# Twenty output stores of a hybrid attention layer issued by GpSimd instead of the sync engine

## The chip, the cores and the metric

The kernel runs on one core of a Trainium2 chip. A core has five engines that run side by side, each with its own instruction queue that is worked off in order: TensorE (PE, matrix products and transpositions), VectorE (DVE), ScalarE (ACT), GpSimd (POOL), and SyncE (SP), which here does nothing but issue DMA transfers. ACT and POOL can issue DMA transfers too; these stand in the same queue as their arithmetic. Engines wait for each other and for the landing of a transfer through semaphores. The metric is the time of the device for one execution in microseconds (us).

## What is computed

One layer of a diffusion backbone, in float32: 1024 latent tokens with 256 context tokens ahead of them, model width 1024. The normalised and modulated tokens are projected once; four heads run a gated delta rule in both directions, four heads a retention in both directions. Both outputs are normalised and gated, joined, projected by `w_out` and added to x; then follows a SwiGLU feed-forward part (FFN). Cut to what matters here:

```python
o_gdn = rms_norm(o_f + o_b, gdn_norm_g) * jax.nn.silu(z...)
o_ret = head_group_norm(r_f + r_b, ret_norm_g) * jax.nn.silu(rg...)
y = jnp.concatenate([o_gdn.reshape(b, tl, W_GDN), o_ret.reshape(b, tl, W_RET)], axis=-1)
...
x = x + g1 * (y[:, CTX_LEN:] @ w_out[layer])
x = x + g2 * swiglu(modulate(rms_norm(x, norm_ffn_g[layer]), sh2, sc2), w_ffn_in[layer], w_ffn_out[layer])
return rms_norm(x, final_g)
```

## The kernel before

Tokens are held in blocks of 128 (one token per partition): blocks t = 0, 1 are the context, t = 2 to 9 the latent tokens, also called l = t − 2 = 0 to 7. A float32 product is made of three products of rounded parts (`hi*hi`, `lo*hi`, `hi*lo`).

The stages that the change touches run between about 630 and 850 us:

- **The delta-rule scan.** Ten steps, in each a forward block and a backward block (`steps`, `step`). When the second direction reaches a latent block, `gate(l)` squares the sum O on ACT into the tile `yo` (L959), makes the norm's factor, multiplies with the factor and the gate `zg` on DVE back into `yo` (L964), and stores `yo` into the first half of the row block `dy[l]` in HBM (L966): eight stores of 256 KB. `yo` has two buffers, so ACT's squares of a block wait until the store of two blocks before has landed. The loads of `zg` (L664, two buffers) wait for the multiply that reads the old one.
- **The retention.** `rstate` makes the state of a block (`kz` on POOL, L1021; `ru` on PE; `Rf` on DVE, L1031), `turn` the transposed queries and keys `qk` (ACT, L1060 and L1061; POOL, L1065 and L1066), `scores` the masked products `pm`, and `output(t)` the output: PE `ro` (L1081 to L1083), ACT copies it into `oc` (L1085), DVE takes the head statistics (`bst`), ACT normalises (L1096, one operation for each head), POOL multiplies with the gate (L1099), and the result is stored into the second half of `dy[t - 2]` (L1100). The blocks t = 2 to 5 run between the scan's steps and are stored from POOL; t = 6 to 9 run after it (`forward_tail`, here called the tail) and are stored from SP. In the rows below these four are oc_8171, oc_8252, oc_8333 and oc_8383.
- **The output projection.** `op_y(l)` loads both halves of `dy[l]` into `yt` (L664, two buffers), transposes them on PE (`yT`, L1187) and splits them into `yhi` (ACT) and `ylo` (DVE). `op_mm` multiplies with the parts of `w_out` (`wohi`, `wolo` and, for the second half of the columns, the tiles b11, t1 and so on; L1201 to L1203) and puts `x1` = x + g1·(y w_out) together on DVE (L1204, L1205). `op_norm(l)` stores `x1` into `dx1[l]` (L1211, 512 KB, read again at the very end of the kernel), takes its squares, and scales `x1` in place: the first half on DVE (L1215), the second on ACT (L1216). Both wait until the store has landed. PE then transposes `x1` (`x1T`, L1223), and its parts are combined on POOL for the FFN (L1237 and L1240, a burst of nine products for a block of the second half).
- **The FFN** begins with `ws` on POOL (L1315) and the split of the weights on ACT and DVE (`whi` L344, `wlo` L345).

The order of the instructions on each engine isn't written in the code: the framework's scheduler works it out with a timeline of its own before the kernel is built. Within an engine's queue the order is then fixed. An instruction that goes to another engine therefore also changes the order of its neighbours, on all engines.

Of the kernel before, what the change touches and what calls it, by code (L numbers as in the profile page):

```python
# [38 lines left out]
def build(nc, tc, ap, dbg=None, stop=None, marks=None):  # L39
    root = ExitStack()  # L40
    V, S, G, T, SY = nc.vector, nc.scalar, nc.gpsimd, nc.tensor, nc.sync
# [45 lines left out]
    def bank(tag, name):  # L87
        return PS["pool"].tile([P, 512], F32, tag=tag, name=name, bufs=PS["tags"][tag])

    def bank_a(name):  # L90
        return bank("pa", name)
# [99 lines left out]
    try:  # L191
# [698 lines left out]
        dy = dr.tile([LT, P, D], F32, tag="dy", name="dy")  # L890
# [62 lines left out]
        def gate(l):  # L953
            zg = zgs.pop(l)
            ssq = SC.tile([P, H], F32, tag="ssq", name="ssq")
            nqe = SC.tile([P, H], F32, tag="nqe", name="nqe")
            yo = SC.tile([P, H, P], F32, tag="yo", name="yo", bufs=2)
            for h in range(H):
                S.activation(yo[:, h, :], O[:, l, h, :], AF.Square, accum_out=ssq[:, h:h + 1])  # L959
            V.tensor_scalar(nqe, nq[:, l, :], P * EPS, P * EPS * EPS, ALU.mult, ALU.add)  # L960
            V.scalar_tensor_tensor(ssq, ssq, 1.0 / P, nqe, ALU.mult, ALU.add)
            rr = rsqrt_mean(SC, None, H, "rg", 0, ssq)
            for h in range(H):
                V.scalar_tensor_tensor(yo[:, h, :], O[:, l, h, :], rr[:, h:h + 1], zg[:, h * P:(h + 1) * P],  # L964
                                       ALU.mult, ALU.mult)
            SY.dma_start(dy[l, :, 0:512], yo.rearrange("p h v -> p (h v)"))  # L966

        zgs = {}

# [107 lines left out]
        def output(t, vv, gt, qk, pm, cur, tail):  # L1077
            po = bank_a("ro")
            for h in range(H):
                hs = slice(h * P, (h + 1) * P)  # L1080
                T.matmul(po[:, hs], qk[:, 2, h, :], cur[:, h, :], start=True, stop=False)  # L1081
                T.matmul(po[:, hs], qk[:, 3, h, :], rb[t][:, h, :], start=False, stop=False)
                T.matmul(po[:, hs], pm[:, h, :], vv[:, hs], start=False, stop=True)  # L1083
            oc = RT.tile([P, H, P], F32, tag="oc", name="oc", bufs=5)
            S.activation(oc.rearrange("p h v -> p (h v)"), po, AF.Copy)  # L1085
            bst = RT.tile([P, H, 6], F32, tag="bst", name="bst", bufs=2)
            mv = RT.tile([P, H, 2], F32, tag="mv", name="mv", bufs=2)
            for h in range(H):
                V.bn_stats(bst[:, h, :], oc[:, h, :])
            for h in range(H):  # L1090
                V.bn_aggr(mv[:, h, :], bst[:, h, :])
            rs = rsqrt_mean(RT, mv[:, :, 1], H, "rr", 1.0)
            nm_ = RT.tile([P, H], F32, tag="nm", name="nm", bufs=2)
            V.scalar_tensor_tensor(nm_, mv[:, :, 0], -1.0, rs, ALU.mult, ALU.mult)
            for h in range(H):
                S.activation(oc[:, h, :], oc[:, h, :], AF.Identity,  # L1096
                             bias=nm_[:, h:h + 1], scale=rs[:, h:h + 1])
            yf = oc.rearrange("p h v -> p (h v)")
            G.tensor_tensor(yf, yf, gt, ALU.mult)  # L1099
            (SY if tail else G).dma_start(dy[t - 2, :, 512:1024], yf)  # L1100

        def forward(t, cur):
            kk, vv, gt, qk = turn(t, False)
# [41 lines left out]
        def xhi(n, q, k=slice(0, 4)):  # L1145
            return X[n][:, 0, q, k, :]

        def xlo(n, q, k=slice(0, 4)):
            return X[n][:, 1, q, k, :]
# [25 lines left out]
        dx1 = dr.tile([LT, P, D], F32, tag="dx1", name="dx1")  # L1175
# [32 lines left out]

        def op_norm(l, y, tr=("pc", "pc")):
            _, _, xl, x1 = y  # L1210
            SY.dma_start(dx1[l], x1)  # L1211
            ssx = OP.tile([P, 1], F32, tag="ssx", name="ssx")
            S.activation(xl, x1, AF.Square, accum_out=ssx)
            rs = rsqrt_mean(OP, ssx, 1, "r1", D)
            V.tensor_scalar(x1[:, 0:512], x1[:, 0:512], rs, None, ALU.mult)  # L1215
            S.activation(x1[:, 512:1024], x1[:, 512:1024], AF.Copy, scale=rs)  # L1216
            sl = slice((l % 4) * P, (l % 4 + 1) * P)
            for half in range(2):
                pt = bank(tr[half], "x1T")
                hf = OP.tile([P, 4, P], F32, tag="hf", name="hf", bufs=4)  # L1220
                for i in range(4):
                    k = half * 4 + i
                    T.transpose(pt[:, i * P:(i + 1) * P], x1[:, k * P:(k + 1) * P], ident)  # L1223
                for i in range(4):
                    k = half * 4 + i
                    if l % 4 == 3 and i % 2:
                        S.activation(hf[:, i, :], pt[:, i * P:(i + 1) * P], AF.Identity,
                                     bias=ada2[:, 0, k:k + 1], scale=ada2[:, 1, k:k + 1])
                    else:
                        V.tensor_scalar(hf[:, i, :], pt[:, i * P:(i + 1) * P], ada2[:, 1, k:k + 1], ada2[:, 0, k:k + 1],  # L1230
                                        ALU.mult, ALU.add)
                held[l // 4, half] = hf
                e = V if l % 4 == 3 else G

                def part(n, src):
                    S.activation(xhi(n, l % 4), src, AF.Copy)
                    e.tensor_tensor(xlo(n, l % 4), src, xhi(n, l % 4).bitcast(F32), ALU.subtract)  # L1237

                def diff(n, r, p, q, op=ALU.subtract):
                    e.tensor_tensor(r, p, q, op)  # L1240
                    part(n, r)

                if l < 4:
                    part("b11" if half == 0 else "b21", hf)
                elif half == 0:
                    held["t1"] = OP.tile([P, 4, P], F32, tag="hs", name="hs", bufs=1)
                    diff("t1", held["t1"], hf, held[0, 0])
                else:
                    t1, b21, b12 = held["t1"], held[0, 1], held[1, 0]
                    diff("t2", t1, hf, t1)  # L1250
                    diff("t3", b12, hf, b12)
                    diff("t4", b21, b21, t1)
                    part("b22", hf)
# [4 lines left out]
        for i, l in enumerate(pairs):  # L1258
            y = nxt
            if l != 7:  # L1260
                nxt = op_y(pairs[i + 1])
            op_mm(y, int(l == 7))
            if before:
                op_norm(*before)
            op_mm(y, int(l != 7))
            before = l, y
# [281 lines left out]
        for m in (1, 6, 2, 7, 5, 4, 3):  # L1548
            gs = [list(range(j, min(j + 2, FH))) for j in range(4 if m == 1 else 0, FH, 2)]
            tail = 9 if m == 3 else 3  # L1550
# [104 lines left out]
```

## Time and profile before

| | us |
|---|---|
| runs shown | 1476.58, 1484.42, 1475.48 |
| their median | 1476.58 |
| the profiled execution, its own time | 1477.96 |
| its span in the trace | 1476.2 |

The profile is one execution, recorded on the chip. Busy times of the engines are sums over the span; a window gives the same for a stretch of it. A row of a group names the line of the kernel, the engine, the operation, what it writes and reads, how often it runs, and its durations. A row of the waits names who waited for whom, with the total in us, how often, and the longest. The chain of waits follows the last instruction back, at each step to what released it; its rows are start, duration and what ran. `SPq` and `POOLq` are the queues of these engines when they issue a transfer. DMA rows give the KB of one transfer and the median time from issue to landing. The names drop buffer numbers and trailing digits: `dx` is `dx1`, `x` can be `x1`.

### The profile page before, as it was taken

The page shows a single profiled execution, that of the slowest core. Times are in us where ns is not written, and L with a number is a line of the kernel's source. Part 1 is how long each engine was busy: PE and PEld are TensorE (multiplying, and loading weights), DVE is VectorE, ACT ScalarE, POOL GpSimd, SP SyncE. Part 2 cuts the span into 40 slices and gives each one's busy share as a digit, 9 for nine tenths or more (in the row PEclk, how much of TensorE's full clock was granted, in tenths as well). Part 3 has the DMA queues.
Part 4 walks back from the last instruction along what each step waited for, and adds up shares of the span by engine and source line. Part 5 has one row for each costly group of instructions (what it writes and reads, how often), then busy time and mean ns, then how long its engine had stood idle before and what let it go on. Part 6 is the DMA issues. An engine that isn't in the chain of part 4 may idle for free.

```text
span 1476.2 us, 24111 instructions
## 1 busy us (share of the span) xinstructions
PE 1397.2 (95%) x8919; PEld 1199.2 (81%) x8919; DVE 964.6 (65%) x1856; ACT 614.0 (42%) x1326; POOL 590.3 (40%) x501
## 2 busy tenths in 40 slices
PE   7999999986789999899799899999999999999997
PEld 2898888975689999898688688877888888788885
DVE  6566789289792435689676877556555564657477
ACT  5643564587333111245443623233333332444445
POOL 0120010243202344234144688898555552335321
PEclk9999999998899999999899999999999999999999
DMA  9536686688888625996532265674222242776863
GB/s 337 197 105 205 189 249 200 219 264 277 282 216 277 238 76 178 416 341 209 184 125 104 97 238 210 242 264 162 105 97 105 107 151 79 260 260 194 288 216 114
DMA packets 170421, 298.14 MB, mean 202 GB/s; under 512 B 43496, under 2 KB 93880, under 8 KB 165952
## 3 DMA queue, kind: packets, MB, share of 16 engines
q1 hardware_dynamic: 118752, 253.17, 50.2%
q10 hardware_dynamic: 49072, 35.83, 7.8%
q0 software_dynamic: 2480, 7.60, 1.4%
q8 instruction: 70, 1.15, 0.3%
q14 instruction: 47, 0.39, 0.1%
HBM read 206.60 MB, written 89.96 MB: 201 GB/s over the span
## 4 chain that ended last, share of the span: by engine, by line
PE 55%; POOL 6%; DMA 5%; DVE 4%; issue 2%; ACT 2%; SPq 1%; ACTq 0%; POOLq 0%; DVEq 0%
PE ffn L1344 7%; PE ffn L1342 6%; PE ffn L1343 6%; PE fo L1470 4%; PE fo L1469 4%; PE fo L1468 4%; PE tm L371 3%; PE tm L373 3%; PE tm L372 3%; PE op L1203 2%; PE op L1201 2%; PE op L1202 2%; DMA wd<-tw 2%; POOL ws L1315 1%; DMA pk<-sd 1%
## 5 line engine op out<-in xcount | busy, mean ns | idle before, releaser
L371 PE MATMUL tm<-whi,hhi 128*128 128x256 f32 (+1 forms) x704 | 199.5, 287 | 7.7 <-ACT vt L859 3.4
L372 PE MATMUL tm<-wlo,hhi 128*128 128x256 f32 (+1 forms) x704 | 199.3, 285 | 2.4 <-issue 2.0
L373 PE MATMUL tm<-whi,hlo 128*128 128x256 f32 (+1 forms) x704 | 197.7, 285 | 0.0
L371 PEld LDWEIGHTS tm<-whi,hhi 128*128 128x128 f32 x704 | 132.8, 190 | 11.8 <-ACT vt L859 3.6
L1342 PE MATMUL ffn<-t,whi 128*128 128x512 f32 x352 | 136.9, 390 | 1.3 <-ACT whi L344 1.3
L1344 PE MATMUL ffn<-t,wlo 128*128 128x512 f32 x352 | 137.0, 390 | 1.0 <-DVE wlo L345 1.0
L1343 PE MATMUL ffn<-t,whi 128*128 128x512 f32 x352 | 137.0, 389 | 0.0
L372 PEld LDWEIGHTS tm<-wlo,hhi 128*128 128x128 f32 x704 | 133.7, 190 | 2.1 <-issue 0.9
L373 PEld LDWEIGHTS tm<-whi,hlo 128*128 128x128 f32 x704 | 132.8, 190 | 2.6 <-issue 1.8
L344 ACT ACTIVATE whi<-wraw 128x512 fp32r<-128x512 f32 (+2 forms) x98 | 75.1, 771 | 141.4 <-PE ffn L1343 80.5
L344 ACT ACTIVATE whi<-ws 128x512 fp32r<-128x512 f32 x88 | 55.6, 632 | 171.5 <-PE ffn L1343 123.4
L345 DVE TENSOR_TENSOR wlo<-ws,whi 128x512 fp32r<-128x512 f32 x88 | 93.9, 1068 | 47.0 <-ACT whi L344 46.8
L1469 PE MATMUL fo<-wlo,ahi 128*128 128x512 f32 x308 | 120.2, 390 | 2.1 <-DVE wlo L345 2.1
L1468 PE MATMUL fo<-whi,ahi 128*128 128x512 f32 x308 | 119.3, 390 | 0.7 <-ACT ahi L344 0.7
L1470 PE MATMUL fo<-whi,alo 128*128 128x512 f32 x308 | 119.0, 390 | 0.0
L345 DVE TENSOR_TENSOR wlo<-wraw,whi 128x512 fp32r<-128x512 f32 (+2 forms) x92 | 99.4, 1082 | 24.6 <-ACT whi L344 24.6
L1342 PE MATMUL ffn<-b,whi 128*128 128x512 f32 x264 | 103.8, 393 | 4.4 <-ACT whi L344 4.4
L1344 PE MATMUL ffn<-b,wlo 128*128 128x512 f32 x264 | 103.6, 393 | 0.8 <-DVE wlo L345 0.8
L1343 PE MATMUL ffn<-b,whi 128*128 128x512 f32 x264 | 103.4, 392 | 0.0
L612 PE MATMUL b<-hlo,whi 128*128 128x512 f32 (+1 forms) x256 | 94.4, 369 | 0.0
L613 PE MATMUL b<-hhi,wlo 128*128 128x512 f32 (+1 forms) x256 | 94.3, 368 | 0.0
L611 PE MATMUL b<-hhi,whi 128*128 128x512 f32 (+1 forms) x256 | 94.3, 368 | 0.0
(446 smaller groups left out, 3448.1 us busy)
## 6 DMA issues: line engine op xcount, KB each, us to landing
adaw<-ada SPq DMA_DIRECT2D x48, 512.0 KB, 4.4
pk<-sd SPq DMA_DIRECT2D x16, 1536.0 KB, 10.0
wraw<-wfi SPq DMA_DIRECT2D x44, 512.0 KB, 3.7
ar<-ad SPq DMA_DIRECT2D x33, 512.0 KB, 4.7
w<-wfo SPq DMA_DIRECT2D x22, 512.0 KB, 5.7
wd<-tw SPq DMA_DIRECT2D x11, 1024.0 KB, 4.8
ad<-act SPq DMA_DIRECT2D x20, 512.0 KB, 3.0
raw<-wd SPq DMA_DIRECT2D x20, 512.0 KB, 4.9
```

Source lines behind the costliest of these rows:

```text
L344: S.activation(hi, raw, AF.Copy)
L345: e.tensor_tensor(lo, raw, hi.bitcast(F32), ALU.subtract)
L371: T.matmul(o, hhi[:, k, tsl], whi[:, k % 4, :], start=(k == 0), stop=False)
L372: T.matmul(o, hhi[:, k, tsl], wlo[:, k % 4, :], start=False, stop=False)
L373: T.matmul(o, hlo[:, k, tsl], whi[:, k % 4, :], start=False, stop=(k == KT - 1))
L612: T.matmul(o, whi[:, k, :], hl, start=False, stop=False)
L1342: T.matmul(o, whi[:, k, :], xhi(xn, slice(0, 4), k), start=(first and k == 0), stop=False, **kw)
L1343: T.matmul(o, whi[:, k, :], xlo(xn, slice(0, 4), k), start=False, stop=False, **kw)
L1344: T.matmul(o, wlo[:, k, :], xhi(xn, slice(0, 4), k), start=False, stop=(k == 3), **kw)
L1468: T.matmul(po[g][i], ahi[:, ts], whi, start=(j == 0 and not kw), stop=False, **kw)
L1469: T.matmul(po[g][i], ahi[:, ts], wlo, start=False, stop=False, **kw)
L1470: T.matmul(po[g][i], alo[:, ts], whi, start=False, stop=(j == FH - 1), **kw)
```

## The change

Three lines issue their store from GpSimd (`G`) where the sync engine (`SY`) did: all eight stores of `yo`, the four stores of `oc` in the tail, and all eight stores of `x1`. What is stored, and where, stays the same.

```diff
             for h in range(H):
                 V.scalar_tensor_tensor(yo[:, h, :], O[:, l, h, :], rr[:, h:h + 1], zg[:, h * P:(h + 1) * P],
                                        ALU.mult, ALU.mult)
-            SY.dma_start(dy[l, :, 0:512], yo.rearrange("p h v -> p (h v)"))
+            G.dma_start(dy[l, :, 0:512], yo.rearrange("p h v -> p (h v)"))
...
             yf = oc.rearrange("p h v -> p (h v)")
             G.tensor_tensor(yf, yf, gt, ALU.mult)
-            (SY if tail else G).dma_start(dy[t - 2, :, 512:1024], yf)
+            G.dma_start(dy[t - 2, :, 512:1024], yf)
...
         def op_norm(l, y, tr=("pc", "pc")):
             _, _, xl, x1 = y
-            SY.dma_start(dx1[l], x1)
+            G.dma_start(dx1[l], x1)
```

The scheduler's order moves with it. ScalarE, at the end of the scan, around the squares of the last gated block (yo_8081) with `-` for the order before and `+` for the new one:

```order
+L131 ACTIVATE rgs_8056<-ssq_8047 128x4
+L1096 ACTIVATE oc_7953<-oc_7953,nm_7975,rry_7966 128x128 x4
 L1061 ACTIVATE qk_8124<-rkT_8126 128x512
-L131 ACTIVATE rgs_8056<-ssq_8047 128x4
+L1170 ACTIVATE wohi_8445<-woraw_8443,gain_8431 128x512
+L959 ACTIVATE yo_8081,ssq_8079<-O_5439 128x128 x4
 L1060 ACTIVATE qk_8205<-rqT_8206 128x512
-L959 ACTIVATE yo_8081,ssq_8079<-O_5439 128x128 x4
 L1061 ACTIVATE qk_8205<-rkT_8207 128x512
-L1170 ACTIVATE wohi_8445<-woraw_8443,gain_8431 128x512
-L1096 ACTIVATE oc_7953<-oc_7953,nm_7975,rry_7966 128x128 x4
```

The normalising operations of oc_7953 and the first copy of `w_out` (wohi_8445) now stand ahead of the squares of yo_8081, where they stood behind them; a copy of qk_8205 goes behind.

GpSimd, from the last gated block through the tail to the first rows of the projection; dy_5438 and dx1_8525 are the two arrays in HBM:

```order
+L966 DMA dy_5438<-yo_8081 128x512
 L1099 TENSOR_TENSOR oc_8171<-oc_8171,vg_8103 128x512
+L1100 DMA dy_5438<-oc_8171 128x512
 L1099 TENSOR_TENSOR oc_8252<-oc_8252,vg_8122 128x512
+L1100 DMA dy_5438<-oc_8252 128x512
 L1099 TENSOR_TENSOR oc_8333<-oc_8333,vg_8203 128x512
+L1100 DMA dy_5438<-oc_8333 128x512
 L1099 TENSOR_TENSOR oc_8383<-oc_8383,vg_8284 128x512
+L1100 DMA dy_5438<-oc_8383 128x512
+L1211 DMA dx1_8525<-x1_8553 128x1024
+L1211 DMA dx1_8525<-x1_8576 128x1024
```

Each of the tail's four products is now followed by its store, which waits for it; the first two stores of x1 stand ahead of the projection's first products.

GpSimd, in the burst of products that follows the second projected block; x1_8653 and x1_8768 are the third and fourth:

```order
 L1237 TENSOR_TENSOR t1_8423<-hs_8820,t1_8423 128x512
 L1237 TENSOR_TENSOR t3_8424<-hf_8811,t3_8424 128x512
+L1211 DMA dx1_8525<-x1_8653 128x1024
 L1240 TENSOR_TENSOR hs_8820<-hf_8825,hs_8820 128x512
 L1240 TENSOR_TENSOR hf_8708<-hf_8708,hs_8820 128x512
 L1237 TENSOR_TENSOR t2_8422<-hs_8820,t2_8422 128x512
 L1237 TENSOR_TENSOR t4_8426<-hf_8708,t4_8426 128x512
+L1211 DMA dx1_8525<-x1_8768 128x1024
```

The store of x1_8653 now stands between the products of the block before, and waits until these are done; that of x1_8768 stands behind the burst.

TensorE, around the transposition of x1_8653, before:

```order
L1201 MATMUL op_8960<-t4_8426,yhi_8746 128x512
L1202 MATMUL op_8960<-t4_8426,yhi_8746 128x512
L1203 MATMUL op_8960<-t4_8426,ylo_8747 128x512
L1223 MATMUL x1T_8936<-ident_65,x1_8653 128x128 x4
L1223 MATMUL x1T_8948<-ident_65,x1_8653 128x128 x4
L1201 MATMUL op_8960<-b22_8427,yhi_8746 128x512
L1202 MATMUL op_8960<-b22_8427,yhi_8746 128x512
L1203 MATMUL op_8960<-b22_8427,ylo_8747 128x512
L1201 MATMUL op_8960<-wohi_8521,yhi_8746 128x512
L1202 MATMUL op_8960<-wolo_8522,yhi_8746 128x512
L1203 MATMUL op_8960<-wohi_8521,ylo_8747 128x512
```

and with the change:

```order
L1187 MATMUL yT_8991<-ident_65,yt_8989 128x128 x4
L1187 MATMUL yT_9000<-ident_65,yt_8998 128x128 x4
L1201 MATMUL op_9010<-wohi_8445,yhi_8872 128x512
L1202 MATMUL op_9010<-wolo_8446,yhi_8872 128x512
L1203 MATMUL op_9010<-wohi_8445,ylo_8873 128x512
L1201 MATMUL op_9010<-wohi_8451,yhi_8872 128x512
L1202 MATMUL op_9010<-wolo_8452,yhi_8872 128x512
L1203 MATMUL op_9010<-wohi_8451,ylo_8873 128x512
L1201 MATMUL op_9010<-wohi_8457,yhi_8872 128x512
L1223 MATMUL x1T_8936<-ident_65,x1_8653 128x128 x4
L1223 MATMUL x1T_8948<-ident_65,x1_8653 128x128 x4
```

It stood among the products of op_8960. It now stands behind the last six of these, two groups of four transpositions of the next block, and seven products of op_9010.

## The prediction

> **What bounds the kernel now.** I read the page first, then the windows around the 20 stores (the scan's end, the projection, the FFN's start), then TensorE's waits there, then the chain of waits.
>
> From the page:
>
> ```profile
> span 1476.2 us, 24111 instructions
> PE   1397.2 (95%) x8919; PEld 1199.2 (81%) x8919; DVE 964.6 (65%) x1856; ACT 614.0 (42%) x1326; POOL 590.3 (40%) x501
> ```
>
> TensorE (PE) is busy 95% of the span, so a DMA issue is worth something only where PE is idle. The windows say where that is; columns are PE, PEld, DVE, ACT, POOL busy, then the granted clock, DMA share, GB/s:
>
> ```profile
> 660.00:690.00 30.00, 29.86 (x266) 29.48 (x266) 28.56 (x107) 14.81 (x58) 15.03 (x14) 1.00 0.64 201
> 690.00:705.00 15.00, 9.15 (x72) 8.29 (x72) 13.63 (x50) 10.53 (x27) 3.33 (x3) 0.92 0.67 230
> 705.00:715.00 10.00, 8.25 (x50) 7.57 (x49) 6.53 (x27) 4.17 (x10) 1.26 (x1) 0.77 0.90 286
> 715.00:735.00 20.00, 16.44 (x65) 12.96 (x66) 11.21 (x27) 10.11 (x21) 3.83 (x3) 0.83 0.50 166
> 735.00:820.00 85.00, 85.00 (x416) 70.39 (x415) 62.33 (x126) 34.51 (x63) 41.82 (x31) 1.00 0.33 113
> 820.00:850.00 30.00, 24.82 (x107) 19.75 (x107) 24.09 (x38) 19.65 (x36) 15.51 (x11) 0.89 0.26 98
> ```
>
> PE is full until 690 and again from 735 to 820. It idles 5.85 + 1.75 + 3.56 = 11.2 us between 690 and 735 (the retention tail) and 5.2 us between 820 and 850. The clock lost there is worth 1.2 + 2.3 + 3.4 + 3.3 = 10.2 us of those 75 us if it were 1.00 throughout, most of it on time in which PE is idle anyway. What PE waits for between 690 and 735, and the chain through it:
>
> ```profile
> PE yT L1187 <- DMA yt<-dy: 2.8, 2, 1.5
> PE ro L1081 <- DVE Rf L1031: 2.3, 1, 2.3
> PE ro L1083 <- DVE pm L1074: 2.2, 2, 1.7
> ...
> 683.01 7.22 DMA dy<-yo
> 690.25 1.28 ACT yo L959 x8
> ...
> 701.82 1.02 DVE Rf L1031 x4
> 703.89 0.61 DVE pm L1074
> ...
> 723.75 3.28 DMA yt<-dy
> ```
>
> Two stores of the change stand on this chain. The store of yo (two buffers) must land before ACT may write yo again. And yt loads read back what the oc stores wrote, and PE waits 2.8 us for them. The store of x1 shows no such wait on PE.
>
> **The change, part by part.** Prices first: the gate's issues on SP and the oc issues on POOL (ns, min/median/max), whom POOL's wait before them was for, the landing of all L1100 stores, then medians to landing of 256 KB stores between 650 and 705, of the oc stores on SP after it, and of 512 KB stores of act later on.
>
> ```profile
> L966 SPq DMA_DIRECT2D dy<-yo x8: 319/320/459, 631.7 to 703.9; - x8
> L1100 POOL DMA_DIRECT2D dy<-oc x4: 580/580/582, 658.5 to 695.8; - x4
>   POOL dy L1100: 1.2, 4
> DMA to landing us min/median/max: 3.6/4.9/7.5
> dy<-yo SPq DMA_DIRECT2D x6, 256.0 KB, 4.6
> dy<-oc POOLq DMA_DIRECT2D x4, 256.0 KB, 5.5
> dy<-oc SPq DMA_DIRECT2D x4, 256.0 KB, 4.0
> ad<-act SPq DMA_DIRECT2D x20, 512.0 KB, 3.0
> ad<-act POOLq DMA_DIRECT2D x2, 512.0 KB, 3.5
> ```
>
> *Removed:* 20 issues of 0.32 us on SP, 6.4 us. Worth 0: SP waits for data there, and the zg load behind each store needs the buffer that the same DVE multiply (L964) reads, so it can't go earlier without the store.
>
> *Added:* 20 issues of 0.58 us on POOL, 11.6 us, plus 0.30 us before an issue whose data POOL itself has just made (1.2 over 4). POOL is 15.03 of 30 busy at 660–690 and 41.82 of 85 at 735–820, so its queue has room; what counts is what stands at each place. To landing, POOL's path is 0.9 us longer in the same window (5.5 against 4.6), 0.5 longer for 512 KB. Bounds for 256 KB: the longest landing of the L1100 group (7.5, whichever queue it was) against the 4.0, +3.5; below, −0.5, since two medians of six and four stores may differ by that much the other way. I take +0.9, from the row of the same window and size.
>
> *The gate's stores (eight, L966).* Until 690 PE is full and they cost 0. POOL now waits in order behind L964, and kz and qk products for the retention stand behind a store:
>
> ```profile
> SPq L966 <- DVE yo L964: 20.4, 4, 8.1
> 684.00 1.03 POOL L1021 TENSOR_TENSOR kz<-kq,Z 128x512 f32<-128x512 f32 x1 [2.51 <-PE ru L1025]
> 697.16 1.49 POOL L1066 TENSOR_TENSOR qk<-qk,XI 128x512 f32<-128x512 f32 x1 [0.77 <-ACT qk L1060]
> 692.53 1.64 ACT L1096 ACTIVATE oc<-oc,nm,rry 128x128 f32<-128x128 f32 x4
> ```
>
> SP's four waits for that multiply, 20.4 us, are now POOL's wherever POOL gets there early. At the one that matters (the store of 683.01), the kz behind it ran at 684.00, so the wait is covered; the store of yo_8049 (693.41 on SP) stands ahead of the last two qk products, the later of which ran at 697.16: covered too. What the chain sees: the store that released ACT at 690.25 lands 0.26 + 0.3 = 0.6 us later if its 7.22 us stays. Against that, the four L1096 of oc_7953 (1.64 us), which ran behind this wait, now stand ahead of it on ACT. Sum 0.6 − 1.64, −1.0 us. Bounds: −5.9 if the whole idle of 690–705 goes; +2.0 if the L1096 give nothing, landing takes another 0.7, and the wohi copy (0.71, the chain's next ACT operation) that now stands ahead of the gate's copies holds them up.
>
> *The tail's stores (four, L1100).* POOL makes oc itself, so the handover 0.30, the longer issue 0.26 and landing 0.9 stand in series with the yt loads: +1.5 us, on the path, since PE waits for yt twice at 725–728. Bounds 0 (landing −0.5, the rest covered) and +4.1 (landing +3.5).
>
> *The x1 stores (eight, L1211).* L1215 and L1216 overwrite x1, so they wait for landing, and then PE's x1T. Five of the eight stand where POOL is idle or done. Three stand inside a burst of products, as the order shows: x1_8653 and x1_8894 behind the third L1237 after the two L1240, x1_9135 one earlier.
>
> ```profile
> 762.17 0.32 SPq L1211 DMA_DIRECT2D dx<-x  x1
> 790.12 0.32 SPq L1211 DMA_DIRECT2D dx<-x  x1
> 813.78 0.32 SPq L1211 DMA_DIRECT2D dx<-x  x1
> 764.51 1.30 POOL L1237 TENSOR_TENSOR t<-hf,t 128x512 fp32r<-128x512 f32 x1
> 791.22 1.30 POOL L1237 TENSOR_TENSOR t<-hf,t 128x512 fp32r<-128x512 f32 x1
> 814.87 1.28 POOL L1237 TENSOR_TENSOR t<-hs,t 128x512 fp32r<-128x512 f32 x1
> DMA to landing us min/median/max: 2.6/2.7/3.6
> L1215 DVE TENSOR_SCALAR x<-x,r1y x8: 474/986/1579, 743.9 to 832.5; 128x512 f32<-128x512 f32 x8
> 769.87 1.04 PE L1223 MATMUL x1T<-ident,x 128*128 128x128 f32 x8
> 797.36 1.04 PE L1223 MATMUL x1T<-ident,x 128*128 128x128 f32 x8
> 820.97 1.03 PE L1223 MATMUL x1T<-ident,x 128*128 128x128 f32 x8
> ```
>
> With the burst's product ended plus 0.3, the stores start at 766.1, 792.8 and 816.5: 3.9, 2.7 and 2.7 us later than on SP. Landing 2.7 + 0.26 + 0.5 = 3.5 us, then L1215 at up to 1.5: x1 is ready at 771.1, 797.8 and 821.5. PE reaches x1T at 769.87, 797.36 and 820.97, but the new order puts 13, 4 and 3 more of the op products ahead (85 us for 416 rows at 735–820: 0.2 us each), for x1_8653 eight transpositions as well (21 rows): 774.1, 798.2, 821.6. So no stall by a hair; I take +0.3, bounds 0 and +2.5 (a store 0.8 us later at each of the three).
>
> *Sum:* −1.0 + 1.5 + 0.3 = +0.8 us. Against the profiled execution (1477.96 us, its span 1476.2) that is 1478.8; the profiled one lies 1.4 us above the median of the runs shown, 1476.58, so on the median's scale 1477.4. The ends together: −5.9 + 0 + 0 = −5.9 and 2.0 + 4.1 + 2.5 = +8.6, that is 1470.7 to 1485.2.
>
> Two pages of the Trainium skill bear on this. "DMA: Bandwidth & Descriptors", section "Issuing engines are not separate DMA queues", says that DMAs of all issuing engines interleave on the same 16 engines, and another issuer saves only the sequencer's time of issue; by it the removed part is worth at most 20 times an issue, and here, with SP waiting, nothing. "SBUF — State Buffer", section "SBUF: two separate sides", speaks against the change: a DMA issued from GpSimd has its descriptors written by GpSimd, which a VectorE operation in a two-port mode locks out. By that each store that meets such an operation is late by its length; the 580/580/582 row, from a stretch with DVE 95% busy, shows no such stretch of the issue itself, and no row here shows it behind the issue.
>
> **The rivals.**
>
> 1. *Slower: x1 stores stuck in POOL's bursts.* Place: the three late norms and the ones behind them. For it: the start is really 2.7 to 3.9 us later, and a late x1T makes the next burst late, which holds the next store. Against: 0.1 to 3.0 us of room by the sums above, and x1T's order was moved. It decides as soon as a landing at the last two takes 0.1 to 0.4 us more than the 3.5 of the sum. If POOL's landing here were 5.5 (its 256 KB row), 2 us more: stalls of 0, 1.6 and 1.9 us and the like at two others, +7 us: 1485. To be over 1% slower (14.8 us, about what a measurement of this kernel can tell from no change) all eight would have to stall by 1.9 us.
> 2. *Slower: stores starved by VectorE.* L1215 takes 474 to 1579 ns, so DVE and POOL do hold each other up by as much as 1.1 us. If a store's work on POOL pays that each time, six stand on the path (one yo, two oc, three x1): 6.6 us over the sum, 1484. Against it stands the 580/582 row. The skill's rule above is this case.
> 3. *Faster: the tail packs.* The yo store's wait leaves ACT's path and yt loads no longer stand behind stores on SP: the 5.9 us idle of 690–705 goes and half of 715–735's 3.6, with some clock (0.77 to 0.83): −8 to −10 us, 1467. For it: the chain spends 7.22 us in that store; against it: the store still releases the same buffer.
> 4. *Nothing:* the moved rows only shift inside covered time, all three terms 0: 1476.6.
>
> **How the numbers follow.** Forecast with its small terms 0.50, nothing at all 0.15 (both end within a microsecond or two of each other), rival 1 0.12, rival 2 0.08, rival 3 0.15. Predicted 1477.4 us. The range takes in the bounds above and goes down to rival 3's near end: 1468 to 1486. Faster by over 1% would need under 1461.8, more than all idle of the tail: 0.02. Slower by over 1% needs over 1491.3: 0.04, from rivals 1 and 2 together. Within 1%: 0.94.
>
> **What would show it.** Right: POOL issues of about 0.58 us at L966 and L1211; PE full at 735–820; ACT still waiting at yo L959 for dy<-yo; PE's wait at yT a little over 2.8 us. Rival 1 shows as PE idle before x1T or before an FFN product, with L1215 waiting for dx; rival 2 as landings of dy<-yo and dx<-x on POOL well above 5.5 and 3.5; rival 3 as PE idle at 690–735 well under 11.2 us. The forecast is wrong if PE's idle between 690 and 850 moves by more than 8 us either way, or if the re-planned order costs time past 850, where no store of the change stands.

## The result, and the profile after

The changed kernel takes 1485.63 us (median of 20 runs, 1481.58 to 1489.45) against 1479.00 us for the kernel before, run beside it: ratio 1.0048, 95% interval 1.0036 to 1.0059, so 6.6 us slower. The forecast was +0.8 us, to 1477.4, with 1468 to 1486 as its range. The time lies inside the range, at its upper end, and within 1% of before; that nothing measurable would happen was wrong. The prediction took 1% (14.8 us) for about what a measurement can tell; the interval here is ±1.7 us.

The profiled execution of the changed kernel spans 1483.8 us (1476.2 before). Its windows, columns as in the prediction:

```profile
690.00:705.00 15.00, 13.61 (x104) 13.34 (x105) 14.93 (x39) 11.64 (x29) 4.97 (x5) 0.89 0.69 246
705.00:715.00 10.00, 6.33 (x39) 5.74 (x37) 7.62 (x42) 3.35 (x9) 0.71 (x2) 0.83 0.64 193
715.00:735.00 20.00, 13.24 (x47) 10.00 (x48) 12.03 (x30) 10.38 (x23) 7.26 (x8) 0.69 0.51 182
735.00:820.00 85.00, 85.00 (x413) 70.17 (x412) 59.25 (x120) 32.49 (x59) 39.57 (x33) 0.99 0.32 111
820.00:850.00 30.00, 21.24 (x91) 16.84 (x91) 23.06 (x34) 15.48 (x32) 17.60 (x15) 0.83 0.29 106
```

PE is still full from 735 to 820, as forecast: x1T does not stall it. Its idle between 690 and 705 has gone down: ACT's wait of 2.9 us for dy<-yo at L959 is gone in the new order. The idle comes back with interest at 705–735 and at 820–850.

Single executions reach this part of the kernel at different times (634 to 641 us among the runs below, with at most the first of the moved stores ahead of it), so stages are best cut from a row of their own. I cut from the transposition L1058 that starts at 636.42 before and 636.19 after: the first 100 us hold the end of the scan and the tail, the 32 us that begin 183 us behind it the start of the FFN. Before, and then after:

```profile
636.42:736.42 100.00, 88.69 (x667) 83.02 (x666) 80.49 (x285) 50.59 (x144) 34.33 (x31) 0.93 0.70 237
819.42:851.42 32.00, 26.82 (x117) 21.40 (x116) 25.36 (x41) 20.28 (x37) 16.25 (x12) 0.89 0.30 110
```

```profile
636.19:736.19 100.00, 85.59 (x640) 80.28 (x639) 82.84 (x283) 48.84 (x142) 40.42 (x42) 0.90 0.66 237
819.19:851.19 32.00, 23.24 (x101) 18.46 (x100) 24.77 (x37) 16.90 (x34) 18.41 (x15) 0.84 0.27 99
```

PE's idle in the tail went from 100 − 88.69 = 11.3 to 14.4 us, at the FFN's start from 32 − 26.82 = 5.2 to 8.8 us. That is 3.1 + 3.6 = 6.7 us, as much as the measured loss. Two places to explain, then. The waits of the changed kernel between 600 and 860 (total us, times, longest) and the rows of its issues:

```profile
PE yT L1187 <- DMA yt<-dy: 5.0, 3, 3.0
PE ffn L1342 <- ACT b L1236: 4.7, 1, 4.7
PE ffn L1343 <- DVE b L1237: 4.0, 1, 4.0
PE op L1201 <- ACT yhi L1190: 3.1, 1, 3.1
```

Before, these waits were 2.8 us at yT and 1.2 us at L1201; the first FFN product waited 4.4 us (for whi on ACT), the second not at all, the third 0.8 us (for wlo on DVE).

```profile
L1211 POOL DMA_DIRECT2D dx<-x x8: 533/573/573, 749.0 to 831.4; - x8
DMA to landing us min/median/max: 3.1/3.9/5.7
L966 POOL DMA_DIRECT2D dy<-yo x8: 539/582/582, 631.7 to 711.2; - x8
DMA to landing us min/median/max: 3.2/5.0/7.4
```

The issues and landings are as costed (0.57 and 0.58 us; 3.9 us for 512 KB against the 3.5 taken). What failed is not a price of the store.

**The FFN's start.** The timeline before, around the stores of the last two of the eight projected blocks (x1_9135 and x1_9250; columns start, duration, what, and the idle ahead with its releaser):

```profile
816.18 1.24 DVE L139 SCALAR_TENSOR_TENSOR r1y<-r1u,r1y 128x1 f32<-128x1 f32 x1
822.99 1.27 POOL L1315 TENSOR_TENSOR ws<-wraw 128x512 f32<-128x512 f32 x1
825.54 1.27 POOL L1315 TENSOR_TENSOR ws<-wraw 128x512 f32<-128x512 f32 x1 [1.28 <-DMA wraw<-wfi]
827.28 1.77 DVE L345 TENSOR_TENSOR wlo<-wraw,whi 128x512 fp32r<-128x512 f32 x1
829.11 0.80 PE L1344 MATMUL ffn<-b,wlo 128*128 128x512 f32 x1 [0.80 <-DVE wlo L345]
```

and after:

```profile
822.08 0.57 POOL L1211 DMA_DIRECT2D dx<-x  x1
822.15 3.10 DVE L139 SCALAR_TENSOR_TENSOR r1y<-r1u,r1y 128x1 f32<-128x1 f32 x1
822.67 1.31 POOL L1237 TENSOR_TENSOR t<-hf,t 128x512 fp32r<-128x512 f32 x1
823.93 1.30 POOL L1240 TENSOR_TENSOR hs<-hf,hs 128x512 f32<-128x512 f32 x1
831.36 0.57 POOL L1211 DMA_DIRECT2D dx<-x  x1
831.96 2.50 POOL L1315 TENSOR_TENSOR ws<-wraw 128x512 f32<-128x512 f32 x2
832.72 4.74 DVE L345 TENSOR_TENSOR wlo<-wraw,whi 128x512 fp32r<-128x512 f32 x1 [0.46 <-ACT whi L344]
834.41 2.49 POOL L1315 TENSOR_TENSOR ws<-ws,wraw 128x512 f32<-128x512 f32 x2
838.27 0.77 PE L1343 MATMUL ffn<-b,whi 128*128 128x512 f32 x1 [4.03 <-DVE b L1237]
```

Behind each of the two stores VectorE stands still while GpSimd runs one product after the other without a gap: an operation on 128x1 elements ends at 825.25, 0.02 us behind the second product's end (823.93 + 1.30; the third follows after a pause of 0.07 us), and one that took 1.77 us takes 4.74, across all four ws products. The FFN's second product then waits 4.03 us. Before, the same ws products ran with a gap, since they waited for a weight tile, and no store stood ahead of them.

**The tail.** The steps of rgy, which the multiply L964 of the last gated block (yo_8081) needs, before and after:

```profile
694.69 0.19 ACT L131 ACTIVATE rgs<-ssq 128x4 f32<-128x4 f32 x1
699.96 0.14 DVE L139 SCALAR_TENSOR_TENSOR rgy<-rgu,rgy 128x4 f32<-128x4 f32 x1
702.76 1.13 DVE L964 SCALAR_TENSOR_TENSOR yo<-O,rgy,zg 128x128 f32<-128x128 f32 x4
704.29 0.92 SPq L664 DMA_DIRECT2D yt<-dy  x2
```

```profile
697.72 0.20 ACT L131 ACTIVATE rgs<-ssq 128x4 f32<-128x4 f32 x1
709.57 0.12 DVE L139 SCALAR_TENSOR_TENSOR rgy<-rgu,rgy 128x4 f32<-128x4 f32 x1
709.73 1.14 DVE L964 SCALAR_TENSOR_TENSOR yo<-O,rgy,zg 128x128 f32<-128x128 f32 x4
710.90 0.80 SPq L664 DMA_DIRECT2D yt<-dy  x2
711.17 0.58 POOL L966 DMA_DIRECT2D dy<-yo  x1 [11.41 <-DVE rry L139]
```

The root on ACT comes 3.0 us later, and from there VectorE needs 11.9 us to the end of the chain where it needed 5.3: in the new order seven copies of `w_out` (wolo) and twelve statistics of the retention's norms stand between its small steps, where three and four stood. So the last gated block is stored, and the first rows of the projection are read, some 6.6 us later, and PE waits at yT and at its first product.

### The profile page after: what moved, and what is told of

Read it like the earlier page. It is cut to its first block, busy times and chain, and to the rows that moved or that the text cites. A ratio compares the mean times of both kernels' runs of the same rounds, so it can differ in the third digit from the quotient of the medians.

```text
span 1483.8 us, 24125 instructions
## 1 busy us (share of the span) xinstructions
PE 1401.2 (94%) x8919; PEld 1204.9 (81%) x8919; DVE 977.8 (66%) x1856; ACT 614.0 (41%) x1326; POOL 600.6 (40%) x521
## 4 chain that ended last, share of the span: by engine, by line
PE 53%; DMA 8%; POOL 6%; DVE 6%; issue 3%; ACT 3%; SPq 1%; ACTq 0%; POOLq 0%; DVEq 0%
PE ffn L1344 6%; PE ffn L1343 6%; PE ffn L1342 6%; PE fo L1468 4%; PE fo L1469 4%; PE fo L1470 4%; PE tm L371 3%; PE tm L373 3%; PE tm L372 3%; PE op L1203 2%; PE op L1201 2%; PE op L1202 2%; DMA wd<-tw 2%; DMA w<-wfo 1%; POOL tw L1396 1%
## 5 line engine op out<-in xcount | busy, mean ns | idle before, releaser
L345 DVE TENSOR_TENSOR wlo<-wraw,whi 128x512 fp32r<-128x512 f32 (+2 forms) x92 | 103.5, 1127 | 27.9 <-ACT whi L344 27.6
## 6 DMA issues: line engine op xcount, KB each, us to landing
pk<-sd SPq DMA_DIRECT2D x16, 1536.0 KB, 11.6
```

Source lines behind the costliest of these rows:

```text
L345: e.tensor_tensor(lo, raw, hi.bitcast(F32), ALU.subtract)
```

## The experiments

PE's idle in the two windows of each profiled execution, cut from its own L1058 row as above, beside the time. "Over" is both idles less before's 16.5 us; the last column is (ratio − 1) times 1478 us, good to about ±2 us by the intervals. A ratio is one of medians of 10 to 20 runs, an idle comes from a single one of them; that of late_l3 and late_l7 was the slowest of its twelve, that of ws_late the fastest. "New order" is the changed kernel's order of every other instruction, "old order" that of before.

| run | stores on GpSimd, order | idle tail | idle FFN | over | ratio (95%) | us |
|---|---|---|---|---|---|---|
| before | none | 11.3 | 5.2 | | | |
| the change | all 20, new | 14.4 | 8.8 | 6.7 | 1.0048 (1.0036–1.0059) | 7.1 |
| pool_old_order | all 20, old | 11.5 | 8.6 | 3.6 | 1.0038 (1.0022–1.0054) | 5.6 |
| sp_new_order | none, new | 13.6 | 5.6 | 2.7 | 0.9994 (0.9982–1.0006) | −0.9 |
| sp_new_again | the same | 12.9 | 6.0 | 2.3 | 1.0004 (0.9996–1.0013) | 0.6 |
| gate_only | 8 yo, planned anew | 14.6 | 5.5 | 3.6 | 1.0037 (1.0023–1.0050) | 5.5 |
| gate_again | the same | 15.1 | 5.5 | 4.2 | 1.0018 (1.0007–1.0030) | 2.7 |
| x1_only | 8 x1, planned anew | 11.4 | 8.7 | 3.6 | 1.0028 (1.0013–1.0043) | 4.1 |
| tail_only | 4 oc, planned anew | 11.6 | 6.3 | 1.5 | 1.0003 (0.9984–1.0023) | 0.4 |
| gate_old_order | 8 yo, old | 11.5 | 5.6 | 0.6 | 1.0006 (0.9994–1.0017) | 0.9 |
| x1_late_sp | 18: not x1_9135, x1_9250; old | 11.1 | 6.3 | 0.8 | 1.0010 (0.9995–1.0025) | 1.5 |
| late_pool_only | only these two, old | 10.9 | 8.8 | 3.2 | 1.0028 (1.0015–1.0042) | 4.1 |
| late_l3 | only x1_9135, old | 12.0 | 7.0 | 2.5 | 1.0026 (1.0013–1.0040) | 3.8 |
| late_l7 | only x1_9250, old | 13.0 | 7.7 | 4.2 | 1.0025 (1.0011–1.0039) | 3.7 |
| spare_dma | none, old; one 64 KB DMA more | 11.1 | 4.8 | −0.7 | 1.0003 (0.9991–1.0016) | 0.4 |
| ws_late | none, old; ws waits | 11.2 | 5.9 | 0.6 | 1.0013 (0.9997–1.0028) | 1.9 |
| ws_late_dma | the same, one 64 KB DMA more | 10.8 | 7.7 | 2.0 | 1.0011 (0.9997–1.0025) | 1.6 |
| l7_behind | only x1_9250, behind ws; old | 11.2 | 5.7 | 0.5 | 0.9991 (0.9978–1.0004) | −1.3 |
| late_sp_new | 18: not x1_9135, x1_9250; new | 14.9 | 5.5 | 3.9 | 1.0021 (1.0009–1.0033) | 3.1 |
| pool_behind | all 20, x1_9250 behind ws; old | 11.3 | 6.8 | 1.6 | 1.0014 (1.0000–1.0027) | 2.1 |

**The order or the stores?** To keep one of them fixed, a function behind the building of the kernel chains each engine's instructions in a given list of their names; an instruction that has gone to another engine is left out of the list:

```diff
+def pin(nc, tc):
+    made = {i.name: i for b in nc.cur_f.blocks for i in b.instructions}
...
+        row = [i for i in row if i.engine == row[0].engine]
+        for a, b in zip(row, row[1:]):
+            tc.add_manual_dep(b, a.name, info, reason="order")
```

pool_old_order is the changed kernel with the list of before, sp_new_order the kernel before with the list of after.

> The 20 stores on POOL as in the changed kernel, but every other instruction held in the order that it had before on its engine. Theory ORDER (the 7.1 us come from the re-planned order of DVE, ACT and PE, the stores cost next to nothing themselves): ratio to before 0.999 to 1.002, PE's idle between 690 and 735 about 11 to 13 us, first FFN product no more than 1 us later than before. Theory PRICE (POOL's longer issue and landing and the products it holds up cost the 7 us): ratio 1.004 to 1.006 with the old order too. In between, 1.002 to 1.004, both carry a part.

> The stores on SP as before, but every other instruction held in the order that it has in the changed kernel. Theory ORDER: ratio to before 1.004 to 1.006 although no store has moved, first projection product near 719 us and first FFN product near 833 us as in the changed kernel. Theory PRICE: ratio 0.999 to 1.002. The two pinned kernels together split the 7.1 us: their two differences from before should add up to about 7 us.

The order alone is free within 0.1%, the stores alone cost 0.38%. Their differences, −0.9 and 5.6 us, add up to 4.7 and not to the 7 us that were expected, so some 2 us, no more than the error of these figures, would need both together. sp_new_order was measured a second time, since its trace shows idle that its time does not:

> The same kernel as sp_new_order (all 20 stores on the sync queue, the rest in the changed kernel's order), taken again: its trace had 2.3 us more PE idle at the tail than before's, its ratio was 0.9994. If that idle costs what it shows: 1.001 to 1.0025. If the first measurement stands: 0.998 to 1.0005, and the new order alone is free.

1.0004: the new order alone still costs less than 0.13%, with 1.5 to 2.3 us more idle in the tail. These two are the runs in which idle and time agree least.

**Which stores?** One of the three lines of the change alone, order planned anew (for gate_only the line of L966; x1_only that of L1211, tail_only that of L1100):

```diff
-            SY.dma_start(dy[l, :, 0:512], yo.rearrange("p h v -> p (h v)"))
+            G.dma_start(dy[l, :, 0:512], yo.rearrange("p h v -> p (h v)"))
```

> Only the eight yo stores on POOL, the order planned anew. The order of the scan's end changes with it, that of the projection hardly. If the loss at the scan's end (first projection product 5.2 us later than before in the changed kernel) hangs on these stores: ratio 1.002 to 1.004, first projection product 3 to 6 us later. If it hangs on the oc stores: ratio 0.999 to 1.001, and the first product within 1 us of before.

> Only the eight x1 stores on POOL, the order planned anew (the scan keeps its old order). If the late start of the FFN (first to 24th product 3 to 4 us longer in the changed kernel) hangs on these stores: ratio 1.002 to 1.004, the DVE split of the first FFN weights stretched to 2 to 5 us behind POOL's products, and the 24th FFN product 3 to 5 us later than before. If it only came with the scan's shift: ratio 0.999 to 1.001.

> Only the four oc stores of the tail on GpSimd, order planned anew. By the prediction's own term 0 to 4.1 us with +1.5 as its middle: ratio 1.0000 to 1.0028, 1.0010 in the middle. Rival (the tail's stores cost nothing, since the reads that wait for them wait for more than them): 0.999 to 1.0005. PE's wait at yT in this run tells the two apart: over 3.5 us in all by the first, about 2.8 by the second.

Two groups cost, each at its own place of the table: the gate's in the tail, x1's at the FFN's start. The tail's four give 1.0003, PE's wait at yT 3.0 us in all, so the 1.5 us of the prediction are not seen, though the interval would still take them. The gate's stores were then tried in the old order, and gate_only again:

> Only the eight yo stores on POOL, every other instruction in the order of before. With the order planned anew they measured 1.0037. If that came from the new order at the scan's end: 0.999 to 1.001. If from the stores themselves (POOL's issue, landing, products behind them): 1.002 to 1.004, with PE's idle between the first retention rows and the first projection product 2 to 5 us larger.

> The same kernel as gate_only (eight yo stores on GpSimd, order planned anew), taken again, because 1.0037 there and 1.0006 in the order of before disagree by more than the trace explains. If the re-planned order with the gate's stores costs: 1.0025 to 1.005. If the first measurement was off: 0.9995 to 1.002.

In the old order they cost nothing that can be told from no change (1.0006). In the new one 1.0037 and 1.0018, and by the second one's own expectation the first was too high; but both intervals are above 1, and 3.6 and 4.2 us of idle lie between the two times. So it takes both, the stores and the order that the scheduler gives them.

The traces show a place where the two meet. In the new order products of GpSimd stand right behind five of the gate's stores, and beside three of these products falls a small step of VectorE. The first of the three in the changed kernel, and then the same step of VectorE in sp_new_order:

```profile
654.17 0.58 POOL L966 DMA_DIRECT2D dy<-yo  x1 [1.36 <-DVE r L917]
654.32 1.54 DVE L138 TENSOR_TENSOR rru<-rru,rry 128x4 f32<-128x4 f32 x1
656.17 1.26 PE L922 MATMUL Tr<-r,pk 128*128 128x128 f32 x8 [1.04 <-DVE r L917]
```

```profile
652.53 0.82 DVE L138 TENSOR_TENSOR rru<-rru,rry 128x4 f32<-128x4 f32 x1
```

The step ends with the product behind the issue (kz, 654.78 to 655.83), and PE waits 1.04 us at Tr where it waits 0.33 in sp_new_order. Behind the store of 686.29 the step L128 takes 0.77 us against 0.16, and PE's wait at rkT (L1059) grows from 1.55 to 2.15 us; behind the store of yo_8049 (694.88) L961, the first step of yo_8081's norm, takes 1.58 against 0.16. gate_only, gate_again and late_sp_new show the same three durations to 0.01 us and the same waits to 0.02 us, sp_new_again those of sp_new_order; in gate_old_order the three steps take 0.27, 0.16 and 0.16 us. PE's two waits are 1.3 us longer by it, and L964 of yo_8081 starts 2.1 us later than in sp_new_order (73.5 against 71.4 us behind the L1058 row).

**The last two x1 stores.** From pool_old_order and from the kernel before in its own order, with one line each (`l % 4 == 3` picks x1_9135 and x1_9250):

```diff
 # x1_late_sp
-            G.dma_start(dx1[l], x1)
+            (SY if l % 4 == 3 else G).dma_start(dx1[l], x1)
 # late_pool_only
-            SY.dma_start(dx1[l], x1)
+            (G if l % 4 == 3 else SY).dma_start(dx1[l], x1)
```

> As the run with the stores on POOL and the order of before, but the last two x1 stores (blocks 3 and 7) are issued by SP again; 18 stores stay on POOL. Theory LAST STORES (these two hold DVE off behind POOL's products for 3.1 and 4.7 us, and the FFN starts late by it): ratio to before 1.000 to 1.002, no DVE operation of over 2 us between 810 and 850, last projection product to 24th FFN product back from 16.9 to about 13.2 us. Theory EVERYWHERE (each store costs a little): ratio stays at 1.003 to 1.005.

> The counterpart: only the last two x1 stores (blocks 3 and 7) on POOL, the other 18 on SP, order of before. LAST STORES: ratio 1.002 to 1.004, DVE operations of 3.1 and about 4.7 us behind the two issues, last projection product to 24th FFN product about 17 us. EVERYWHERE: ratio 0.999 to 1.001.

Two of the 20 stores carry 0.28%, the other 18 together 0.10% with an interval that includes nothing. No VectorE operation of over 2 us is left in x1_late_sp, as expected; but from the last projection product to the 24th FFN product it takes 15.6 us and not 13.2, so not all of the FFN's late start hangs on these two. One at a time (`l == 7` and `l == 3`):

> Only the store of x1_9250 on GpSimd, everything else on its engine and in its order of before. Of the 1.0028 that both late stores cost together, theory QUEUE puts most at this one, since four ws products in a row follow it: 1.0015 to 1.0030, with a VectorE operation of over 4 us at the start of the FFN. Rival BURST (the other store, inside the burst of products, carries it): 0.999 to 1.001.

> Only the store of x1_9135 on GpSimd, everything else on its engine and in its order of before. Theory QUEUE: 0.9995 to 1.0012, with one tiny VectorE operation (L139) of about 3 us instead of 1.2 as the trace. Rival BURST: 1.0015 to 1.0030, as much as both late stores together.

Each alone costs about as much as both, within the ±2 us, so the second one's price is not added to the first's. The expectation that put little on x1_9135 missed. In late_l3 its store makes the tiny operation take 3.09 us, and lands late:

```profile
820.36 3.09 DVE L139 SCALAR_TENSOR_TENSOR r1y<-r1u,r1y 128x1 f32<-128x1 f32 x1
825.50 0.49 DVE L1215 TENSOR_SCALAR x<-x,r1y 128x512 f32<-128x512 f32 x1 [2.05 <-DMA dx<-x]
826.04 1.10 PE L1223 MATMUL x1T<-ident,x 128*128 128x128 f32 x8 [0.75 <-DVE x L1215]
```

That is the path of the prediction's first rival (L1215 waits for dx, then x1T is late), with 0.75 us of its own on PE; the rest of its 1.8 us stands at the FFN's first products.

**What holds VectorE?** First, one DMA of 64 KB for which nobody waits, from GpSimd, just ahead of the first ws product, in before's order (SPARE holds `ident`):

```diff
+    to = nc.dram_tensor("spare", (P, 1024), F32, kind="Internal").ap()
+    return nc.gpsimd.dma_start(to[:, 0:P], SPARE[0]).ins
```

> The kernel of before with one more DMA and nothing else moved: a 64 KB store of a constant tile into a spare array, issued by POOL right ahead of its first ws product; nobody reads it or waits for it. It adds a store to the work of the reference. If an issue on POOL by itself keeps DVE off for as long as POOL's products follow without a gap: a DVE operation of 2.5 to 5 us behind it, and the 24th FFN product 1 to 4 us later, ratio 1.000 to 1.003. If the stall only comes since the x1 store starts the ws products late, into DVE's weight split: no DVE operation over 2 us there, ratio 0.999 to 1.001.

Nothing: 1.0003. But there ws came 0.57 us behind the issue, since it still waited for its weights, and VectorE's operation took its usual time:

```profile
824.45 0.58 POOL L1652 DMA_DIRECT2D spare<-ident  x1
825.60 1.55 POOL L1315 TENSOR_TENSOR ws<-wraw 128x512 f32<-128x512 f32 x1 [0.57 <-DMA wraw<-wfi]
825.94 1.76 DVE L1237 TENSOR_TENSOR b<-hf,b 128x512 fp32r<-128x512 f32 x1
```

So two runs that differ in the issue alone. In ws_late all stores stay on the sync queue, and the first ws product waits for the last half of x1_9250 as it does behind its store; ws_late_dma issues the spare DMA of `ident` between that wait and the product. I-9585 is the first ws product, I-9445 the last L1205 of x1_9250:

```diff
+    tc.add_manual_dep(made["I-9585"], "I-9445", late, reason="late")
```

> All stores on the sync queue, every engine's instructions in the order of before; only the first ws product of GpSimd (L1315) now waits until VectorE has made the last half of x1_9250 (L1205), as it does where that row's store stands ahead of it on GpSimd. Theory QUEUE (what costs is that GpSimd's products stand behind the waiting store): ws starts some 2 us later than before and then without gaps, since all four weight tiles have landed; one VectorE operation of over 4 us lies across the four products, and the ratio to before is 1.0010 to 1.0030. Rival TRANSFER (it takes a store issued by GpSimd): no VectorE operation over 2.5 us there, ratio 0.999 to 1.001.

> As ws_late (all 20 stores on the sync queue; the first ws product waits for the last half of x1_9250), but between that wait and the product GpSimd issues one DMA of 64 KB of ident to a spare array, for which nobody waits. Theory ISSUE (products that follow an issue on GpSimd without a gap keep VectorE out until the row of them ends): one VectorE operation of over 4 us across the four ws products, ratio 1.0015 to 1.0035. Rival LATE (the late products alone carry the cost): no VectorE operation over 2.5 us there, and a ratio as in ws_late, 1.000 to 1.0025.

ws_late, four products in a row and no issue ahead:

```profile
821.02 2.82 POOL L1315 TENSOR_TENSOR ws<-wraw 128x512 f32<-128x512 f32 x2 [1.63 <-DVE x L1205]
822.62 1.77 DVE L1237 TENSOR_TENSOR b<-hf,b 128x512 fp32r<-128x512 f32 x1 [0.36 <-ACT b L1236]
823.81 3.39 POOL L1315 TENSOR_TENSOR ws<-ws,wraw 128x512 f32<-128x512 f32 x2
```

ws_late_dma, the same with the issue:

```profile
823.88 0.58 POOL L1652 DMA_DIRECT2D spare<-ident  x1 [1.80 <-DVE x L1205]
824.48 2.50 POOL L1315 TENSOR_TENSOR ws<-wraw 128x512 f32<-128x512 f32 x2
825.32 4.65 DVE L1237 TENSOR_TENSOR b<-hf,b 128x512 fp32r<-128x512 f32 x1 [0.37 <-ACT b L1236]
826.94 2.48 POOL L1315 TENSOR_TENSOR ws<-ws,wraw 128x512 f32<-128x512 f32 x2
```

Without the issue the engines take turns: VectorE's operation takes 1.77 us, and GpSimd's four products need 2.82 + 3.39 us. With it GpSimd runs all four in 2.50 + 2.48 us, and VectorE's operation takes 4.65 us. An issue that has nothing to do with the data is enough, if products follow it without a gap. PE's idle at the FFN's start is 7.7 against 5.9 us: its third product waits 3.55 us for wlo where it waits 1.74. The two times, 1.0011 and 1.0013, do not tell these runs apart. The ratio of 1.0015 or more that the expectation gave the hold has not come, and the 1.0013 without a hold lies in the range that the theory with one had given. So what the hold does to VectorE and PE is shown, and its price by itself is not shown by a time; the idle says some 2 us.

The remedy at the same place: x1_9250's store from GpSimd, but behind the four ws products. In GpSimd's list, I-9463 is the store and I-9644 the fourth product:

```diff
+        if row[0].engine == made["I-9463"].engine:
+            row.insert(row.index(made["I-9644"]) + 1, made["I-9463"])
```

> As late_l7 (only the store of x1_9250 on GpSimd), but it stands behind the first four ws products instead of ahead of them. Theory ISSUE: no VectorE operation over 2.5 us at the start of the FFN, since the products no longer follow an issue; ws runs early as in before; the store starts some 4 us late, so the row behind it is overwritten late, and what that costs shows as waits for dx: ratio 0.999 to 1.0015. Rival TRANSFER (a store that GpSimd issues costs at this place whatever its position): 1.002 to 1.003.

```profile
826.40 3.41 POOL L1315 TENSOR_TENSOR ws<-ws,wraw 128x512 f32<-128x512 f32 x2
826.91 1.76 DVE L345 TENSOR_TENSOR wlo<-wraw,whi 128x512 fp32r<-128x512 f32 x1
829.75 0.58 POOL L1211 DMA_DIRECT2D dx<-x  x1
```

0.9991 against late_l7's 1.0025, with intervals that do not meet: the same store on the same engine costs nothing that shows when it stands four products further on. This undoes both effects of the place, the wait ahead of ws and the hold behind the issue. The same insertion with all 20 stores on GpSimd (pool_behind), and the line of x1_late_sp in the new order (late_sp_new):

> All 20 stores on GpSimd and every other instruction in the order of before, as pool_old_order (1.0038), but x1_9250's store stands behind the first four ws products. Theory ISSUE: PE's idle at the start of the FFN falls from 8.6 us to 5 to 7 us (what is over 5.2 would be the burst behind x1_9135's store), no VectorE operation over 4 us there, and the ratio is 1.000 to 1.002. Rival (the issue ahead of ws is not what counts among 20 stores): idle 8 to 9 us and 1.003 to 1.005.

> The changed kernel with x1_9135's and x1_9250's stores back on the sync queue, every other instruction in the changed kernel's own order: 18 stores on GpSimd. Theory: the two late stores carry 0.0028 of the 1.0048, so 1.001 to 1.003 is left, as at the gate. Rival (in the new order the gate's stores take all, as gate_only's 1.0037 has it): 1.0035 to 1.005.

pool_behind takes back about 3.5 of pool_old_order's 5.6 us (1.0014; the intervals overlap slightly) and keeps x1_9135's hold. late_sp_new keeps the tail's part, 14.9 us of idle there and 5.5 at the FFN. No version beats the kernel before beyond its interval.

## Why the prediction was wrong

- *Removed issues, 0:* nothing speaks against it. No run with stores taken off SP is below before's time by more than its interval (the lowest is 0.9991).
- *Issue and landing:* right, to 0.01 us for the issue and 0.4 us for 512 KB.
- *The x1 stores, +0.3 with bounds 0 and +2.5:* this step failed, and the larger part of the loss is here. The room at x1T was read rightly, PE is full to 820. But the term asked only when the store lands. It did not ask what stands behind the issue on GpSimd: the row of ws products for the FFN's weights and, across it, VectorE's operations. 820–850 had been read as one of the two places where PE idles, yet no term was made for it; x1_9250's store, the last one, stood among the "five of the eight where POOL is idle or done". It waits for x1_9250 there with the ws products behind it. Measured +3.6 us of idle, and 4.1 us of time for the two late stores alone (late_pool_only), past the upper bound.
- *The gate's stores, −1.0, and the tail's, +1.5:* together +0.5, measured +3.1 us of idle. The −1.64 for the moved L1096 was there in part: ACT's wait at yo L959 is gone, and the idle of 690–705 fell by 4.5 us. What the step left out is VectorE's order: it bounded the wohi copies on ACT at 0.71 us, but the norm of yo_8081 goes through four small VectorE steps, between which the new order puts other rows, and these cost 6.6 us. gate_old_order and gate_only show that it is this order together with the stores. "Until 690 PE is full and they cost 0" failed too: from the L1058 row to 690 PE idles 2.6 us, where it idled 0.1. And of the products behind a gate's store the step asked whether they come late, not whom they hold: three of these stores hold VectorE as the late x1 stores do. The tail's own four stores gave 1.0003, so the +1.5 is not seen.
- *The range:* that 1485.63 lies inside it is luck. Its upper end is a sum of bounds (2.0 + 4.1 + 2.5), of which the x1 stores' was passed and the tail's, the largest, stayed unused.
- *Rival 1, 1485:* it and rival 2 (1484) came close in time, and it named an FFN product as the sign. (Its own sum, 1477.4 + 7, gives 1484.4.) Its mechanism, landings too late for x1T, is seen at x1_9135 in late_l3 with 0.75 us on PE, and not as the 7 us that it priced; in the changed kernel x1T does not wait.
- *Rival 2, stores starved by VectorE:* the other way round. The issues stay at 0.53 to 0.58 us, and VectorE is the one that is held. The Trainium skill, "SBUF — State Buffer", section "SBUF: two separate sides", calls the port that both share an exclusive lock, held for a whole instruction by whichever engine starts first. ws_late agrees, with VectorE in after one product; behind an issue the 4.65 us over four products do not.
- *What was to show it:* "PE's idle between 690 and 850 moves by more than 8 us" was too wide a sign. It moved by 4.2 us (16.3 to 20.6), another 2.4 us came ahead of 690, and the loss was already there.

Two things stay open. The new order by itself costs no time that can be told, though L964 of yo_8081 starts 71.4 us behind the L1058 row in sp_new_order against 66.3 before: 5 of the 7 us by which it is late with the stores on GpSimd (73.5 in gate_only) belong to the order. The other 2 go with the steps of VectorE that are held behind the gate's stores; whether these are all of the 2.7 to 5.5 us that gate_only and gate_again cost, no run shows, since none keeps the stores and the new order and takes the hold away. And how the hold and the wait ahead of ws share the price at the FFN's start.

## What to carry to other kernels

A store moved to an engine that also computes is priced by what stands behind it in that engine's queue, and by whom these instructions hold up; the store's own issue and landing were the small part here. Where it must go there, place it behind the row of products and not ahead of it: one store moved by four instructions was worth 0.3%. And where a scheduler re-plans, read the new order on every engine of the chain, the small steps of a norm above all.

## What the runs showed of the hardware

- Behind a DMA issue on GpSimd with products following without a gap, a VectorE operation waited through the row of them: 3.09 to 3.10 us for 128x1 elements (1.24 before), 4.65 to 4.74 us for 128x512 (1.76 to 1.77 without the issue), in eight traces. It needed no data dependence (ws_late_dma) and vanished with a gap of 0.57 us (spare_dma). Not every operation waited: beside the product behind the store of 680.92 in the changed kernel, L1031 took its usual 0.34 us, and beside the first ws product of ws_late_dma L128 its usual 0.15. Why, the trace does not show.
- GpSimd's products are the faster for it: four ws products took 6.2 us beside VectorE in ws_late and 5.0 us behind the issue in ws_late_dma, with VectorE held.
- The clock granted in the FFN's 32 us goes in steps with PE's idle there: 0.95 at 4.8 us of idle (spare_dma), 0.89 at 5.2 to 6.3 us (ten runs, before among them), 0.84 at 6.3 to 8.8 us (nine). So a longer stall at this place came with a lower clock as well.
